# A second token half prepared behind four output sums: a transformer layer on one Trainium2 core

## The chip, the core and the metric

The kernel runs on one core of one Trainium2 chip. The metric is device time in microseconds of one execution. Engines are named as in the profile: PE (TensorE, matmuls and transposes), PEld (its weight loads), DVE (VectorE), ACT (ScalarE), POOL (GpSimd), SP (SyncE); the last two and ACT also issue DMAs. L124 is line 124 of the kernel before.

## The reference

One encoder layer over 1024 tokens of width 1024, in float32:

```python
h   = x + concat(windowed attention, gated delta rule)(rmsnorm(x) @ w_in) @ w_out
hn  = rmsnorm(h, norm_ffn_w)
h   = h + square(relu(hn @ w_ffn_in)) @ w_ffn_out      # 1024 -> 4096 -> 1024
out = rmsnorm(h, norm_final_w)
```

The change lies between the product with `w_out` and the first products of the feed-forward part, and in the last rows of the final norm. What comes before is not touched.

## The kernel before

**Numbers.** Every float32 operand of a large product is split into a high and a low part (a cast on ACT, then a subtraction on POOL or DVE), and a product is three matmuls (`mm3`, L124, L125, L126) that add into one PSUM bank of 128x512. There are eight banks: four named psA and four named psB.

**Output sums.** Tokens are cut into eight chunks of 128. `out_all` walks them from 7 down to 0. For each, `out_gdn` prepares the gated part (four squares L899, small steps L901 to L905, a scaled copy L906, four small transposes L909, a product with the weight L910, a split L119 and L120), `out_gemm` multiplies it with `w_out` (24 matmuls into two psA banks) and adds it to the chunk's rows `h[c]` (L875), and the rows are saved to DRAM as `hd[c]` (L925) and appended to `summed`.

**Token halves.** The feed-forward products are formed in the Strassen-Winograd way: tokens, inner width and columns are each cut in two, and seven products P1 to P7 stand in for eight. The token operand has eight blocks of 128 inner columns per token half: upper blocks k = 0 to 3 and lower blocks 4 to 7. B11 and B21 are the first half's upper and lower blocks, b12 and B22 the second half's. The combinations T3, N1, T2 and N4 are made from them. `norm_rows` gets a chunk's rows ready (a square with its sum on ACT L203, 1/root on POOL L190 and L191, a scaling on DVE L205). `token_block` transposes one block of four chunks into one psB bank (L209), and `split_rows` reads the bank twice (ACT L214, DVE L215). `operand` splits a combination (ACT L948, then POOL or DVE L949).

`tokens_second` does the second half (chunks 4 to 7): per k an upper block, copied to b12 (L963), and a lower one, split to B22 and combined to T3 (L969). `tokens_first` does the first half (chunks 0 to 3): per k an upper block (B11, then N1 = block - b12 at L983), two additions in SBUF that make T2 (L987, L988), then the lower block (B21, and N4 = block - T2 at L991).

**Columns.** `columns` loads two blocks of `w_ffn_in` for a group of 256 columns, forms the sums S1 to S4 and splits what each product needs. Groups 0 and 1 are early ones: P7 and P3, which need only the second half, are taken at once, and the rest later by `rest`. Group 0's raw weights and sums share tiles.

**Order.** A scheduler sets each engine's order from the order in which the code is written and from its own model of times; `weave` mixes generators by weights. In `output`, chunk sums run alone until six are done, then the rest of the sums is mixed with `tokens_second`. Then the first half's rows are normalised, group 1's columns are taken, and the early products are mixed with `tokens_first`. After that, all 16 column groups and the second feed-forward product run in steady state.

**End.** `second_products` adds the last products to the rows of the output and calls `finish` for each of them (square L1212, 1/root, scaling L1215, save L1216). Row 7's last half goes through `finish_last` (L1196 to L1206), which works on half rows and saves them from two queues.

Of the kernel before, what the change touches and what calls it, by code (L numbers as in the profile page):

```python
# [77 lines left out]
class Block:  # L78
# [852 lines left out]
    def norm_h(self, c):  # L931
        self.rows[c] = self.norm_rows(self.h[c], self.sc((P, D)))

# [19 lines left out]
    def tokens_second(self):  # L953

        nc = self.nc
        self.norm_half(1)
        yield 0.5
        rows = [self.rows[4 + i] for i in range(4)]
        self.b12 = []
        for k in range(4):  # L960
            ps = self.token_block(rows, k)
            b12 = self.pt()
            nc.scalar.activation(out=b12, in_=ps, func=AF.Copy, scale=self.w_ffn[:, k:k + 1])  # L963
            self.b12.append(b12)
            yield 0.5
            ps = self.token_block(rows, 4 + k)
            self.split_rows(ps, self.w_ffn, 4 + k, self.X["B22"])
            t3 = self.pt()
            nc.vector.scalar_tensor_tensor(out=t3, in0=ps, scalar=self.w_ffn[:, 4 + k:5 + k], in1=b12, op0=ALU.mult,  # L969
                                           op1=ALU.subtract)  # L970
            self.operand("T3", t3, k % 2)
            yield 0.5

    def tokens_first(self):

        nc = self.nc
        rows = [self.rows[i] for i in range(4)]
        w = self.w_ffn
        for k in range(4):
            ps = self.token_block(rows, k)  # L980
            self.split_rows(ps, w, k, self.X["B11"])
            n1, t2, n4 = self.pt(), self.pt(), self.pt()
            nc.vector.scalar_tensor_tensor(out=n1, in0=ps, scalar=w[:, k:k + 1], in1=self.b12[k], op0=ALU.mult,  # L983
                                           op1=ALU.subtract)
            yield 0.5
            b22 = self.X["B22"][k]
            nc.vector.tensor_tensor(out=t2, in0=n1, in1=b22[:, 0].bitcast(F32), op=ALU.add)  # L987
            nc.vector.tensor_tensor(out=t2, in0=t2, in1=b22[:, 1].bitcast(F32), op=ALU.add)  # L988
            ps = self.token_block(rows, 4 + k)
            self.split_rows(ps, w, 4 + k, self.X["B21"])  # L990
            nc.vector.scalar_tensor_tensor(out=n4, in0=ps, scalar=w[:, 4 + k:5 + k], in1=t2, op0=ALU.mult,  # L991
                                           op1=ALU.subtract)
            self.operand("T2", t2, False)
            self.operand("N1", n1, False)
            self.operand("N4", n4, True)
            yield 0.5

    def load_w1(self, g):
# [5 lines left out]

    def columns(self, raws, early=False):

# [16 lines left out]
        if early:  # L1023
            take("P7")
        take("P1", "P2")
        a["S2"], a["S4"] = a["A11"], a["A12"]
        v.scalar_tensor_tensor(out=a["S2"], in0=a["S1"], scalar=-1.0, in1=a["A11"], op0=ALU.mult, op1=ALU.subtract)
# [133 lines left out]
    def second_products(self, n, p, left, right, banks, last):  # L1161
# [5 lines left out]
        for i in range(4):  # L1167
# [15 lines left out]
            if last and p == "P6":  # L1183
                for d in (self.h[i][:, hi], self.h[4 + i][:, hi], self.h[4 + i][:, lo]):
                    nc.gpsimd.tensor_tensor(out=d, in0=d, in1=u2, op=ALU.add)
            if last and p in ("P3", "P4"):
                self.finish(i if p == "P3" else 4 + i)

    def finish_last(self, t, ps):
# [5 lines left out]
        scr, hw, o = self.pt((P, HALF), BF16), [self.pt(), self.pt()], [self.pt(), self.pt()]  # L1195
        nc.scalar.activation(out=scr, in_=h[:, hi], func=AF.Square, accum_out=ss[:, 1:2])  # L1196
        nc.gpsimd.tensor_tensor(out=hw[1], in0=h[:, hi], in1=self.w_fin[:, hi], op=ALU.mult)
        nc.vector.tensor_tensor(out=h[:, lo], in0=h[:, lo], in1=ps, op=ALU.add)
        nc.scalar.activation(out=scr, in_=h[:, lo], func=AF.Square, accum_out=ss[:, 0:1])
        nc.vector.tensor_tensor(out=hw[0], in0=h[:, lo], in1=self.w_fin[:, lo], op=ALU.mult)  # L1200
        nc.vector.tensor_tensor(out=ss[:, 0:1], in0=ss[:, 0:1], in1=ss[:, 1:2], op=ALU.add)
        self.rstd(ss[:, 0:1], rs)
        nc.scalar.activation(out=o[0], in_=hw[0], func=AF.Copy, scale=rs)
# [33 lines left out]
    def phases(self):  # L1237
# [42 lines left out]
        def output():  # L1280
            yield from self.attention()
            yield from self.out_attn()
            cols[0], rest[0] = self.columns(self.load_w1(0), True)
            out = self.out_all(range(NT - 1, -1, -1))
            while len(self.summed) < 6:
                yield next(out)
            yield from weave((out, 20.0), (self.tokens_second(), 12.0))
# [7 lines left out]
        self.norm_half(0)  # L1295
        cols[1], rest[1] = self.columns(self.load_w1(1), True)
        run(weave((chain(self.early(cols[0]), self.early(cols[1])), 10.0), (self.tokens_first(), 12.0)))
# [23 lines left out]
        for g in range(ng):  # L1321
            then = {}
            if g == 0:
                rest[1]("P6", "P5", "P4")
            elif g + 1 < ng:
                cols[g + 1] = self.columns(self.load_w1(g + 1))
            else:
                w2[0] = self.load_second(0, 0)
                then = {"P2": lambda: prepare(0), "P6": after_p6, "P3": after_p3}
# [31 lines left out]
```

## Time and profile before

| | us |
|---|---|
| median of three runs | 1262.61 |
| lowest and highest run | 1261.38, 1266.63 |
| profiled execution | 1267.07 |
| its span from first to last instruction | 1265.4 |
| PE busy | 1210.0 (96%) |
| DVE, ACT, POOL busy | 859.0, 621.4, 577.7 |

The granted clock of PE over the whole span was 0.983 of full speed. Times of single instructions below are of the profiled execution, in us from its start. In a row of the trace stand start, duration, engine, line, operation, and what it writes and reads; in brackets the idle time before it and the instruction that ended it. Duration of a pipelined matmul is longer than the distance between two starts.

The output sums of the last chunks end at about 605, the first half's blocks at about 645. The first feed-forward product ends at about 905, the second at 1257, and the rest to 1265.4 is the final norm.

### The profile page before, as it was taken

How to read it: one execution, taken by the hardware profiler on the slowest of the kernel's cores; microseconds unless marked ns; L12 is line 12 of the kernel's file. 1: busy time of each engine (PE TensorE's matmuls, PEld its weight loads, DVE VectorE, ACT ScalarE, POOL GpSimd, SP SyncE). 2: the span in 40 equal slices, each digit the busy share in tenths (PEclk: the TensorE clock that was granted, in tenths of full speed). 3: DMA queues.
4: the chain of work that ended last, by engine and by line, in shares of the span. 5: the costliest groups of instructions: out<-in, count | busy, mean ns of one | idle time of the engine just before them, and what ended most of it. 6: DMA issues, size and time to landing. Idle time of an engine off the chain costs nothing.

```text
span 1265.4 us, 18552 instructions
## 1 busy us (share of the span) xinstructions
PE 1210.0 (96%) x6482; PEld 970.6 (77%) x6482; DVE 859.0 (68%) x1534; ACT 621.4 (49%) x1347; POOL 577.7 (46%) x486
## 2 busy tenths in 40 slices
PE   6999999999899999999799999999999999999997
PEld 5778777778767778878578787887777888888885
DVE  5667666882378987684774544545577897887976
ACT  6455688244475653122654544545545444443443
POOL 5354221352422324143565535445354665565595
PEclk9999999899889999999999999999999999999999
DMA  6134444332956658224034443444687624434233
GB/s 236 51 120 136 111 156 156 122 124 55 229 146 162 174 181 324 68 82 134 18 125 142 153 163 132 152 142 156 204 278 280 220 102 166 150 113 155 85 99 133
DMA packets 121630, 187.62 MB, mean 148 GB/s; under 512 B 11043, under 2 KB 64416, under 8 KB 121537
## 3 DMA queue, kind: packets, MB, share of 16 engines
q1 hardware_dynamic: 96708, 152.58, 37.4%
q10 hardware_dynamic: 16381, 29.67, 6.2%
q0 software_dynamic: 8448, 4.20, 1.8%
q8 instruction: 51, 0.84, 0.3%
q14 instruction: 42, 0.34, 0.1%
HBM read 122.39 MB, written 63.49 MB: 147 GB/s over the span
## 4 chain that ended last, share of the span: by engine, by line
PE 58%; DVE 7%; DMA 3%; issue 2%; POOL 1%; ACT 1%; ACTq 0%; POOLq 0%; DVEq 0%
PE psA L124 8%; PE psA L125 8%; PE psA L126 8%; PE psB L126 7%; PE psB L124 7%; PE psB L125 7%; PE psB L796 5%; DMA pg<-sd 2%; PE psA L584 2%; PE psA L573 2%; DVE pg L1137 1%; PE psA L544 1%; DVE pt L1146 1%; POOL pg L120 1%; PE psA L545 1%
## 5 line engine op out<-in xcount | busy, mean ns | idle before, releaser
L124 PE MATMUL psA<-pg,wh 128*128 128x512 f32 x416 | 167.9, 404 | 2.7 <-ACT pt L458 2.2
L126 PE MATMUL psA<-pg,wl 128*128 128x512 f32 x416 | 167.0, 401 | 0.0
L125 PE MATMUL psA<-pg,wh 128*128 128x512 f32 x416 | 166.6, 400 | 0.3 <-POOL pg L949 0.3
L120 POOL TENSOR_TENSOR wl<-wr,wh 128x512 fp32r<-128x512 f32 x44 | 70.7, 1629 | 153.3 <-ACT wh L119 153.2
L1137 DVE TENSOR_TENSOR pg<-pg 128x512 fp32r<-128x512 f32 x112 | 123.2, 1135 | 18.1 <-ACT pg L1136 18.1
L120 POOL TENSOR_TENSOR wh<-wr,wh 128x512 fp32r<-128x512 f32 x32 | 47.6, 1508 | 132.1 <-ACT wh L119 124.4
L1054 ACT ACTIVATE pt<-pt 128x512 f32<-128x512 f32 x64 | 40.4, 632 | 123.0 <-DVE pt L1044 123.0
L125 PE MATMUL psA<-pg,pg 128*128 128x512 f32 x256 | 99.8, 391 | 0.4 <-POOL pg L120 0.4
L124 PE MATMUL psA<-pg,pg 128*128 128x512 f32 x256 | 99.0, 391 | 0.9 <-DVE pg L1182 0.9
L126 PE MATMUL psA<-pg,pg 128*128 128x512 f32 x256 | 99.7, 389 | 0.0
L120 POOL TENSOR_TENSOR pg<-wr,pg 128x512 fp32r<-128x512 f32 x48 | 73.4, 1559 | 50.8 <-ACT pg L119 50.8
L124 PEld LDWEIGHTS psA<-pg,wh 128*128 128x128 f32 x416 | 79.3, 191 | 22.1 <-ACT pt L458 2.4
L125 PEld LDWEIGHTS psA<-pg,wh 128*128 128x128 f32 x416 | 79.2, 190 | 20.4 <-issue 0.9
L126 PEld LDWEIGHTS psA<-pg,wl 128*128 128x128 f32 x416 | 79.1, 190 | 18.5
L1136 ACT CAST pg<-pg 128x512 fp32r<-128x512 f32 x112 | 66.8, 620 | 38.4 <-DMA pg<-sd 32.0
L125 PE MATMUL psB<-pg,pg 128*128 128x512 f32 x192 | 75.8, 395 | 1.5 <-POOL pg L120 1.4
L126 PE MATMUL psB<-pg,pg 128*128 128x512 f32 x192 | 75.7, 394 | 1.2 <-DVE pg L1137 1.2
L124 PE MATMUL psB<-pg,pg 128*128 128x512 f32 x192 | 75.3, 393 | 0.7 <-ACT pg L1136 0.7
L119 ACT CAST wh<-wr 128x512 fp32r<-128x512 f32 x76 | 43.5, 623 | 45.2 <-PE psA L125 23.6
L1044 DVE TENSOR_TENSOR pt<-psB,pt 128x512 f32<-128x512 f32 x39 | 26.9, 689 | 52.7 <-PE psB L126 30.3
L1044 DVE TENSOR_TENSOR pt<-psA,pt 128x512 f32<-128x512 f32 x39 | 26.7, 689 | 52.8 <-PE psA L126 37.4
L124 PEld LDWEIGHTS psA<-pg,pg 128*128 128x128 f32 x256 | 48.0, 188 | 12.6 <-DVE pg L1182 2.2
(379 smaller groups left out, 3329.5 us busy)
## 6 DMA issues: line engine op xcount, KB each, us to landing
sd<-pt ACTq DMA_DIRECT2D x112, 256.0 KB, 2.1
pg<-sd SPq DMA_DIRECT2D x112, 256.0 KB, 2.8
wr<-in_w_ffn_in SPq DMA_DIRECT2D x32, 512.0 KB, 3.7
wr<-in_w_in SPq DMA_DIRECT2D x22, 512.0 KB, 4.9
pg<-in_x SPq DMA_DIRECT2D x16, 512.0 KB, 4.6
wr<-in_w_ffn_out SPq DMA_DIRECT2D x16, 512.0 KB, 4.9
sc<-kvd SPq DMA_DIRECT2D x14, 512.0 KB, 4.4
kvd<-pt SPq DMA_DIRECT2D x16, 256.0 KB, 2.8
```

The costliest lines, as they stand in the source:

```text
L119: nc.scalar.copy(out=h, in_=raw)
L120: (eng or nc.gpsimd).tensor_tensor(out=l, in0=raw, in1=h.bitcast(F32), op=ALU.subtract)
L124: nc.tensor.matmul(ps, wh, xh, start=first, stop=False, skip_group_check=onto)
L125: nc.tensor.matmul(ps, wh, xl, start=False, stop=False, skip_group_check=onto)
L126: nc.tensor.matmul(ps, wl, xh, start=False, stop=last, skip_group_check=onto)
L573: nc.tensor.transpose(ps[:, g, :], tiles[g // 2][:, g % 2, j * P:(j + 1) * P], self.ident)
L584: nc.tensor.matmul(ps[64 * kv:64 * kv + 64, :], self.va[:, kb, 64 * kv:64 * kv + 64], pts[kv][j].rearrange("p g q -> p (g q)"), start=j == ...
L796: nc.tensor.matmul(ps[:, h - g.start, :], left(h), right[:, h, :], start=True, stop=True)
L1044: self.nc.vector.tensor_tensor(out=out, in0=in0, in1=in1, op=ALU.add)
L1054: self.nc.scalar.activation(out=c, in_=c, func=AF.Relu)
L1136: nc.scalar.copy(out=s[:, 0], in_=raw)
L1137: v.tensor_tensor(out=s[:, 1], in0=raw, in1=s[:, 0].bitcast(F32), op=ALU.subtract)
```

## The change

Four parts.

1. In `output`, the second half joins the sums when four are done (chunks 7 to 4, all that it needs). Its rows are normalised in place in `h` instead of in a copy, so the scaling has to come after the save to DRAM. b12 and t3 of one k lie in one tile of double width and are kept.
2. `tokens_first` takes all four upper blocks first. T2 is made from PSUM and the kept t3 in one pass. The lower blocks follow, and the splits of N4 come last, alternately on POOL and DVE.
3. For group 1, S2 and S4 get tiles of their own, and the splits for P1 and P2 move to the later call.
4. Row 6's `finish` moves into `finish_last`, behind row 7's 1/root; the 1/root of row 7 is made from two partial sums on POOL.

```diff
--- before.py
+++ after.py
@@ -929,7 +929,7 @@
 
 
     def norm_h(self, c):
-        self.rows[c] = self.norm_rows(self.h[c], self.sc((P, D)))
+        self.rows[c] = self.norm_rows(self.h[c], self.sc((P, D)) if c < 4 else None)
 
     def norm_half(self, half):
         for c in range(4 * half + 3, 4 * half - 1, -1):
@@ -956,19 +956,20 @@
         self.norm_half(1)
         yield 0.5
         rows = [self.rows[4 + i] for i in range(4)]
-        self.b12 = []
+        self.b12, self.t3 = [], []
         for k in range(4):
+            both = self.pg((P, 2, HALF))
+            b12, t3 = both[:, 0], both[:, 1]
             ps = self.token_block(rows, k)
-            b12 = self.pt()
             nc.scalar.activation(out=b12, in_=ps, func=AF.Copy, scale=self.w_ffn[:, k:k + 1])
-            self.b12.append(b12)
             yield 0.5
             ps = self.token_block(rows, 4 + k)
             self.split_rows(ps, self.w_ffn, 4 + k, self.X["B22"])
-            t3 = self.pt()
             nc.vector.scalar_tensor_tensor(out=t3, in0=ps, scalar=self.w_ffn[:, 4 + k:5 + k], in1=b12, op0=ALU.mult,
                                            op1=ALU.subtract)
             self.operand("T3", t3, k % 2)
+            self.b12.append(b12)
+            self.t3.append(t3)
             yield 0.5
 
     def tokens_first(self):
@@ -976,24 +977,27 @@
         nc = self.nc
         rows = [self.rows[i] for i in range(4)]
         w = self.w_ffn
+        t2, n4 = [], []
         for k in range(4):
             ps = self.token_block(rows, k)
             self.split_rows(ps, w, k, self.X["B11"])
-            n1, t2, n4 = self.pt(), self.pt(), self.pt()
+            n1, t = self.pt(), self.pt()
+            nc.vector.scalar_tensor_tensor(out=t, in0=ps, scalar=w[:, k:k + 1], in1=self.t3[k], op0=ALU.mult, op1=ALU.add)
             nc.vector.scalar_tensor_tensor(out=n1, in0=ps, scalar=w[:, k:k + 1], in1=self.b12[k], op0=ALU.mult,
                                            op1=ALU.subtract)
+            self.operand("N1", n1, False)
+            t2.append(t)
             yield 0.5
-            b22 = self.X["B22"][k]
-            nc.vector.tensor_tensor(out=t2, in0=n1, in1=b22[:, 0].bitcast(F32), op=ALU.add)
-            nc.vector.tensor_tensor(out=t2, in0=t2, in1=b22[:, 1].bitcast(F32), op=ALU.add)
+        for k in range(4):
             ps = self.token_block(rows, 4 + k)
             self.split_rows(ps, w, 4 + k, self.X["B21"])
-            nc.vector.scalar_tensor_tensor(out=n4, in0=ps, scalar=w[:, 4 + k:5 + k], in1=t2, op0=ALU.mult,
+            n4.append(self.pt())
+            nc.vector.scalar_tensor_tensor(out=n4[k], in0=ps, scalar=w[:, 4 + k:5 + k], in1=t2[k], op0=ALU.mult,
                                            op1=ALU.subtract)
-            self.operand("T2", t2, False)
-            self.operand("N1", n1, False)
-            self.operand("N4", n4, True)
+            self.operand("T2", t2[k], False)
             yield 0.5
+        for k in range(4):
+            self.operand("N4", n4[k], k % 2)
 
     def load_w1(self, g):
         return self.load_w(self.w_cols(self.io["w_ffn_in"][0], 256 * g, 256))
@@ -1002,7 +1006,8 @@
                 "P5": ("S1", "N1", "sc"), "P7": ("S3", "T3", "wh"), "P3": ("S4", "B22", "wl"),
                 "P4": ("A22", "N4", "sc")}
 
-    def columns(self, raws, early=False):
+    def columns(self, raws, early=0):
+
 
 
         nc, v = self.nc, self.nc.vector
@@ -1022,8 +1027,11 @@
         v.tensor_tensor(out=a["S3"], in0=a["A11"], in1=a["A21"], op=ALU.subtract)
         if early:
             take("P7")
-        take("P1", "P2")
-        a["S2"], a["S4"] = a["A11"], a["A12"]
+        if early == 2:
+            a["S2"], a["S4"] = self.pt((P, 4, P)), self.pt((P, 4, P))
+        else:
+            take("P1", "P2")
+            a["S2"], a["S4"] = a["A11"], a["A12"]
         v.scalar_tensor_tensor(out=a["S2"], in0=a["S1"], scalar=-1.0, in1=a["A11"], op0=ALU.mult, op1=ALU.subtract)
         v.tensor_tensor(out=a["S4"], in0=a["A12"], in1=a["S2"], op=ALU.subtract)
         if early:
@@ -1183,7 +1191,7 @@
             if last and p == "P6":
                 for d in (self.h[i][:, hi], self.h[4 + i][:, hi], self.h[4 + i][:, lo]):
                     nc.gpsimd.tensor_tensor(out=d, in0=d, in1=u2, op=ALU.add)
-            if last and p in ("P3", "P4"):
+            if last and p in ("P3", "P4") and (p, i) != ("P4", 2):
                 self.finish(i if p == "P3" else 4 + i)
 
     def finish_last(self, t, ps):
@@ -1194,12 +1202,15 @@
         ss, rs = self.small((P, 2)), self.small((P, 1))
         scr, hw, o = self.pt((P, HALF), BF16), [self.pt(), self.pt()], [self.pt(), self.pt()]
         nc.scalar.activation(out=scr, in_=h[:, hi], func=AF.Square, accum_out=ss[:, 1:2])
+        nc.gpsimd.tensor_scalar(out=ss[:, 1:2], in0=ss[:, 1:2], scalar1=1.0 / D, scalar2=EPS, op0=ALU.mult, op1=ALU.add)
         nc.gpsimd.tensor_tensor(out=hw[1], in0=h[:, hi], in1=self.w_fin[:, hi], op=ALU.mult)
         nc.vector.tensor_tensor(out=h[:, lo], in0=h[:, lo], in1=ps, op=ALU.add)
         nc.scalar.activation(out=scr, in_=h[:, lo], func=AF.Square, accum_out=ss[:, 0:1])
         nc.vector.tensor_tensor(out=hw[0], in0=h[:, lo], in1=self.w_fin[:, lo], op=ALU.mult)
-        nc.vector.tensor_tensor(out=ss[:, 0:1], in0=ss[:, 0:1], in1=ss[:, 1:2], op=ALU.add)
-        self.rstd(ss[:, 0:1], rs)
+        nc.gpsimd.tensor_scalar(out=ss[:, 0:1], in0=ss[:, 0:1], scalar1=1.0 / D, scalar2=ss[:, 1:2], op0=ALU.mult,
+                                op1=ALU.add)
+        nc.gpsimd.tensor_tensor(out=rs, in0=ss[:, 0:1], in1=self.nhalf_exp[:, :1], op=ALU.pow)
+        self.finish(6)
         nc.scalar.activation(out=o[0], in_=hw[0], func=AF.Copy, scale=rs)
         nc.vector.tensor_scalar(out=o[1], in0=hw[1], scalar1=rs, scalar2=None, op0=ALU.mult)
         for i, sl in enumerate((lo, hi)):
@@ -1280,9 +1291,9 @@
         def output():
             yield from self.attention()
             yield from self.out_attn()
-            cols[0], rest[0] = self.columns(self.load_w1(0), True)
+            cols[0], rest[0] = self.columns(self.load_w1(0), 1)
             out = self.out_all(range(NT - 1, -1, -1))
-            while len(self.summed) < 6:
+            while len(self.summed) < 4:
                 yield next(out)
             yield from weave((out, 20.0), (self.tokens_second(), 12.0))
 
@@ -1293,7 +1304,7 @@
                          self.scan(1, tt[1], w_gdn)), 95.0)))
         ng = DFF // 256
         self.norm_half(0)
-        cols[1], rest[1] = self.columns(self.load_w1(1), True)
+        cols[1], rest[1] = self.columns(self.load_w1(1), 2)
         run(weave((chain(self.early(cols[0]), self.early(cols[1])), 10.0), (self.tokens_first(), 12.0)))
         rest[0]("P6", "P5", "P4")
         steps = [(n, p) for n in range(ng // 4) for p in SECOND]
@@ -1321,7 +1332,7 @@
         for g in range(ng):
             then = {}
             if g == 0:
-                rest[1]("P6", "P5", "P4")
+                rest[1]("P1", "P2", "P6", "P5", "P4")
             elif g + 1 < ng:
                 cols[g + 1] = self.columns(self.load_w1(g + 1))
             else:
```

TensorE has the same matmuls and transposes as before. What moves is shown at three places, as each engine's list of instructions (line, operation, output and inputs with the tile's number; the line numbers are those of the kernel that the list is from).

PE at the end of chunk 3's sum, first before, then changed. pg_5261, pg_5165, pg_5076 and pg_4973 are the rows of chunks 4, 5, 6 and 7; psA_5984 and psA_6046 are the bank of chunk 2's sum, pt_5870 and pt_5871 its split operand.

```order
L126 MATMUL psA_5943<-pg_5039,pt_5816 128x512
L909 MATMUL psA_5974<-ident,wr_5959 128x128 x4
L124 MATMUL psA_5984<-pg_5224,pt_5870 128x512
L125 MATMUL psA_5984<-pg_5225,pt_5870 128x512
L126 MATMUL psA_5984<-pg_5224,pt_5871 128x512
L124 MATMUL psA_5984<-pg_4936,pt_5870 128x512
```

```order
L126 MATMUL psA_5943<-pg_5039,pt_5816 128x512
L209 MATMUL psB_5986<-ident,pg_5261 128x128
L209 MATMUL psB_5986<-ident,pg_5165 128x128
L209 MATMUL psB_5986<-ident,pg_5076 128x128
L209 MATMUL psB_5986<-ident,pg_4973 128x128
L209 MATMUL psB_5992<-ident,pg_5261 128x128
...
L209 MATMUL psB_6112<-ident,pg_5076 128x128
L209 MATMUL psB_6112<-ident,pg_4973 128x128
L909 MATMUL psA_6036<-ident,wr_6021 128x128 x4
L124 MATMUL psA_6046<-pg_5224,pt_5870 128x512
```

All 32 transposes of the second half stand behind chunk 3's sum, ahead of the small transposes and the sum of chunk 2; before, they stood further back among the matmuls.

ACT at the same place in the changed kernel. The first row casts chunk 1's gated part, L203 squares the rows of chunks 7 to 3, L899 are chunk 0's four squares, and L964 copies an upper block to b12.

```order
L119 CAST pt_5925<-wr_5903 128x512
L203 ACTIVATE pt_5959,sm_5957<-pg_4973 128x1024
L203 ACTIVATE pt_5966,sm_5964<-pg_5076 128x1024
L203 ACTIVATE pt_5973,sm_5971<-pg_5165 128x1024
L203 ACTIVATE pt_5980,sm_5978<-pg_5261 128x1024
L203 ACTIVATE pt_6015,sm_6013<-pg_5350 128x1024
L899 ACTIVATE scr_6025,sm_6023<-pg_3794 128x128 x2
L964 ACTIVATE pg_5985<-psB_5986,cols 128x512
L899 ACTIVATE scr_6025,sm_6023<-pg_3794 128x128
L214 ACTIVATE pg_5997<-psB_5992,cols 128x512
L899 ACTIVATE scr_6025,sm_6023<-pg_3794 128x128
```

The squares of the second half follow the cast directly, and chunk 0's preparation lies between the first evictions.

DVE in the first half, before (one k) and changed (upper blocks). In the changed kernel L985 makes T2 and L986 makes N1, and pg_5985 and pg_6004 hold the kept b12 and t3.

```order
L215 SCALAR_TENSOR_TENSOR pg_6287<-psB_6282,cols,pg_6287 128x512
L983 SCALAR_TENSOR_TENSOR pt_6290<-psB_6282,cols,pt_6098 128x512
L215 SCALAR_TENSOR_TENSOR pg_6301<-psB_6296,cols,pg_6301 128x512
L987 TENSOR_TENSOR pt_6291<-pt_6290,pg_6128 128x512
L988 TENSOR_TENSOR pt_6291<-pt_6291,pg_6128 128x512
L991 SCALAR_TENSOR_TENSOR pt_6292<-psB_6296,cols,pt_6291 128x512
L949 TENSOR_TENSOR pg_6311<-pt_6292,pg_6311 128x512
L215 SCALAR_TENSOR_TENSOR pg_6319<-psB_6314,cols,pg_6319 128x512
```

```order
L215 SCALAR_TENSOR_TENSOR pg_6243<-psB_6238,cols,pg_6243 128x512
L985 SCALAR_TENSOR_TENSOR pt_6247<-psB_6238,cols,pg_5985 128x512
L986 SCALAR_TENSOR_TENSOR pt_6246<-psB_6238,cols,pg_5985 128x512
L215 SCALAR_TENSOR_TENSOR pg_6258<-psB_6253,cols,pg_6258 128x512
L985 SCALAR_TENSOR_TENSOR pt_6262<-psB_6253,cols,pg_6004 128x512
L986 SCALAR_TENSOR_TENSOR pt_6261<-psB_6253,cols,pg_6004 128x512
L215 SCALAR_TENSOR_TENSOR pg_6273<-psB_6268,cols,pg_6273 128x512
L985 SCALAR_TENSOR_TENSOR pt_6277<-psB_6268,cols,pg_6072 128x512
```

Before, a k had two L215, N1, two additions, N4 and a split; now an upper block has three passes over the same bank. On ACT the changed order there is:

```order
L214 ACTIVATE pg_6243<-psB_6238,cols 128x512
L948 CAST pg_6250<-pt_6246 128x512
L214 ACTIVATE pg_6258<-psB_6253,cols 128x512
...
L948 CAST pg_6265<-pt_6261 128x512
L214 ACTIVATE pg_6273<-psB_6268,cols 128x512
L948 CAST pg_6280<-pt_6276 128x512
L214 ACTIVATE pg_6288<-psB_6283,cols 128x512
L948 CAST pg_6295<-pt_6291 128x512
```

The cast of N1 (L948) stands ahead of the next block's first eviction (L214).

DVE in the last rows, before and changed (L1215 and L1226 are the scaling of a row in `finish`, L1200 and L1209 the product with the norm's weight in `finish_last`):

```order
L1182 TENSOR_TENSOR pg_8769<-pg_8769,psA_11070 128x512
L1215 SCALAR_TENSOR_TENSOR wr_11255<-pg_8768,sm_11250,wl_10676 128x1024
L1198 TENSOR_TENSOR pg_8770<-pg_8770,psA_11084 128x512
L1215 SCALAR_TENSOR_TENSOR wr_11277<-pg_8769,sm_11272,wl_10676 128x1024
L1200 TENSOR_TENSOR pt_11295<-pg_8770,wl_10676 128x512
L1201 TENSOR_TENSOR sm_11292<-sm_11292 128x1
L1204 TENSOR_SCALAR pt_11298<-pt_11296,sm_11293 128x512
```

```order
L1190 TENSOR_TENSOR pg_8759<-pg_8759,psA_11060 128x512
L1226 SCALAR_TENSOR_TENSOR wr_11245<-pg_8758,sm_11240,wl_10666 128x1024
L1207 TENSOR_TENSOR pg_8760<-pg_8760,psA_11074 128x512
L1209 TENSOR_TENSOR pt_11276<-pg_8760,wl_10666 128x512
L1215 TENSOR_SCALAR pt_11279<-pt_11277,sm_11274 128x512
L1226 SCALAR_TENSOR_TENSOR wr_11294<-pg_8759,sm_11289,wl_10666 128x1024
```

Row 6's scaling, which stood between row 7's sum and its product, is now the last one.

## The prediction

> **What bounds the kernel now.** I read the page first (busy shares), then the waits of TensorE by stage, then the instructions in time order around the place that the change touches, then the granted clock there and the last rows.
>
> ```profile
> PE 1210.0 (96%) x6482; PEld 970.6 (77%) x6482; DVE 859.0 (68%) x1534; ACT 621.4 (49%) x1347; POOL 577.7 (46%) x486
> ```
>
> TensorE is the bound: 96% of the span. A change that leaves its instructions alone can gain only where it idles or runs slowly. The order of TensorE's instructions differs in one stretch, from the end of chunk 3's output sum (585.11) to product P1 of column group 2 (660.98). Its rows, its windows (us, busy of PE, PEld, DVE, ACT, POOL, then granted clock, DMA share, GB/s) and TensorE's waits in it:
>
> ```profile
> 585.46 0.48 PE L124 MATMUL psA<-pg,pt 128*128 128x512 f32 x1
> ...
> 600.19 1.91 PE L209 MATMUL psB<-ident,sc 128*128 128x128 f32 x16
> 601.85 0.47 PE L124 MATMUL psA<-pg,pt 128*128 128x512 f32 x1
> ```
> ```profile
> 585.11:609.00 23.89, 23.89 (x123) 19.59 (x121) 13.28 (x20) 11.80 (x21) 8.70 (x13) 1.00 0.38 133
> 609.00:640.00 31.00, 21.38 (x86) 14.58 (x86) 24.94 (x34) 19.39 (x35) 21.77 (x19) 0.89 0.10 31
> 640.00:660.80 20.80, 20.80 (x92) 16.84 (x91) 13.19 (x18) 10.25 (x19) 10.35 (x8) 1.00 0.38 130
> ```
> ```profile
> PE psB L124 <- DVE pt L983: 2.5, 1, 2.5
> PE psB L209 <- DVE pt L991: 2.1, 1, 2.1
> PE psB L209 <- DVE sc L205: 2.0, 2, 1.2
> PE psA L124 <- ACT wl L119: 1.4, 1, 1.4
> ```
>
> Between 585.46 and 600.19 stand 63 matmuls, 0.234 us each; sixteen transposes take 1.66, 0.104 each. The stretch holds 228 matmuls, 64 transposes and a group of four small ones (0.35): 53.3 + 6.7 + 0.35 = 60.3 us of work in 75.9. So 15.5 us are lost, and that is all the change can win there. Idle are 9.6 (31.00 − 21.38), all between 609 and 640, where the first token half is evicted from PSUM; DVE is busy 24.94 of those 31. The clock of 0.89 costs 3.4 more (31 × 0.11); the other 2.5 are stretched matmuls beside transposes and short waits. From 585 to 609 TensorE loses nothing visible: second-half preparation lies beside the output sums.
>
> **Second half after four sums.** The 32 transposes of the second half move from between later matmuls to one block right behind chunk 3's sum, ahead of chunks 2, 1 and 0. The first of them reads chunk 4, the last normalised. On ACT the four squares (L203) follow a cast (L119) that waited for DVE until 580.68.
>
> ```profile
> 580.68 0.62 ACT L119 CAST pt<-wr 128x512 fp32r<-128x512 f32 x1 [5.32 <-DVE wr L910]
> ...
> 593.17 1.05 ACT L203 ACTIVATE pt<-pg 128x1024 bf16<-128x1024 f32 x1
> 594.13 0.19 ACT L203 ACTIVATION_READ_ACCUMULATOR pt<-pg 128x1 f32 x1
> ```
> ```profile
> 589.71 0.75 POOL L190 TENSOR_SCALAR sm<-sm 128x1 f32<-128x1 f32 x1
> ...
> 594.73 0.19 POOL L190 TENSOR_SCALAR sm<-sm 128x1 f32<-128x1 f32 x1
> 595.01 0.55 POOL L191 TENSOR_TENSOR sm<-sm,nhalf_exp 128x1 f32<-128x1 f32 x1
> ```
> ```profile
> 595.59 0.75 DVE L205 TENSOR_SCALAR sc<-pg,sm 128x1024 f32<-128x1024 f32 x1 [0.79 <-POOL sm L191]
> ```
>
> Squares start at 581.2 and, at 1.05 each, end at 585.4. From the accumulator's end (594.32) to the normalised row (596.34) the trace has 2.0. So the row is ready at 587.4, and TensorE, done at 585.11, idles 2.3. POOL's small L190 took 0.75 beside a running L205 instead of 0.19; with two such hits, and a queue behind the split of group weights, it is up to 3.7. I take 3.0 (gap A). Before, gap A was hidden by chunks 3 to 0, 15 us of matmuls; that cover is now behind the transposes in TensorE's queue.
>
> Normalising in place makes L205 wait for the save of the row to DRAM:
>
> ```profile
> 580.01 0.33 SPq L925 DMA_DIRECT2D hd<-pg  x1
> ```
> ```profile
> hd<-pg SPq DMA_DIRECT2D x8, 512.0 KB, 3.0
> ```
>
> The save of chunk 4 lands at 583.0, over 3 us ahead of its L205 (586.7): nothing. Were it as late as 588, chunks 5 to 7 would be behind it on DVE, and gap A would grow by 1.
>
> Eight blocks of transposes follow each other on four psB banks, with no matmul between. Block b5 needs b1's bank back, and so on; each needs the ACT copy and two DVE passes:
>
> ```profile
> 601.41 0.68 ACT L214 ACTIVATE pg<-psB,cols 128x512 fp32r<-128x512 f32 x1
> ```
> ```profile
> 602.13 0.75 DVE L215 SCALAR_TENSOR_TENSOR pg<-psB,cols,pg 128x512 fp32r<-128x512 f32 x1 [1.75 <-ACT pg L214]
> 602.79 0.74 DVE L969 SCALAR_TENSOR_TENSOR pt<-psB,cols,pt 128x512 f32<-128x512 f32 x1
> ```
> ```profile
> L899 ACT ACTIVATE scr<-pg x32: 303/310/313, 473.4 to 572.2; 128x128 f32<-128x128 f32 x32
> ```
>
> b6 waits for DVE on b2, b8 for DVE on b4. ACT has chunk 0's four L899 among them (0.31 each, some 0.44 with the accumulator read, 0.19, partly beside it), and DVE four small L901 to L904. Pairs follow at some 2.0 (ACT: 0.58 + 0.58 + cast 0.52 + L899 0.44). Four pairs, 8.0 us from the first transpose to the first matmul of chunk 2, hold 3.7 of work: 4.3 lost (gap B; 3.3 without the L899, 4.9 with every DVE op in the way). This too was covered by matmuls before.
>
> The shared slot for b12 and t3 takes no instruction. DVE's normalisation in place reads and writes the same bytes: nothing.
>
> **First half by upper blocks.** T2 comes from one pass over PSUM with t3 (L985) in place of two SBUF additions (L987, L988): four DVE passes fewer, net of what N4 shifts. Order on DVE is now L215, L985, L986 per upper block, and ACT goes L948 (cast N1 of block k), then L214 of block k+1: the next eviction waits for L986 of this one. Cycle: cast 0.52, L214 0.69, DVE 3 × 0.66 + 0.08, hand-overs 0.08: 3.35 per upper block. Four take 13.4, and four lower ones at about 1.4 (two DVE passes; their cast is early) 5.6: 19.0. Before, the cycle is read from L983, once per k:
>
> ```profile
> 618.58 0.74 DVE L983 SCALAR_TENSOR_TENSOR pt<-psB,cols,pt 128x512 f32<-128x512 f32 x1
> ...
> 632.04 0.73 DVE L983 SCALAR_TENSOR_TENSOR pt<-psB,cols,pt 128x512 f32<-128x512 f32 x1
> ...
> 639.60 0.73 DVE L983 SCALAR_TENSOR_TENSOR pt<-psB,cols,pt 128x512 f32<-128x512 f32 x1
> ```
>
> Three cycles take 21.0, 7.0 each: four are 28.0, 9.0 more.
>
> TensorE, though, has little to do meanwhile. From 585.11 it has gaps A and B (7.3), 36 transposes (3.7) and 98 matmuls (22.9) before this half's first block: 619.0. The eviction of b1 begins at 619.9, so b4's bank is free only at 619.9 + 13.4 less the first cast = 632.7. The blocks b1 to b4 and the 22 matmuls behind them last to 625.8; then all four lower blocks stand in one row of transposes, 1.7, done at 627.5 without waits, and b8 waits for 632.7: 5.2 (gap C; 3.9 with b7's wait partly before, 5.6). Then P1's 12 matmuls and P2's first nine (4.9) cover the lower evictions but for the last: 1.2, with a little for POOL's low parts (gap D; 0 to 4.0). POOL's price depends on what DVE does meanwhile:
>
> ```profile
> 632.54 1.30 POOL L120 TENSOR_TENSOR sc<-wr,sc 128x512 fp32r<-128x512 f32 x1
> 633.79 1.73 POOL L120 TENSOR_TENSOR sc<-pt,sc 128x512 fp32r<-128x512 f32 x1
> ```
> ```profile
> 633.35 1.03 DVE L987 TENSOR_TENSOR pt<-pt,pg 128x512 f32<-128x512 f32 x1
> ```
>
> POOL now gets 12 low parts instead of 10 (N4 two, no longer all on DVE). I take 1.45 per row, near the 1.30, which stands beside DVE's PSUM pass of 632.04; most DVE passes beside the new low parts read PSUM too. The Trainium skill, "SBUF — State Buffer", section "SBUF: two separate sides", has DVE and GpSimd exclude each other for a whole instruction when DVE has two SBUF inputs; L985 has one. The 1.73, beside the SBUF addition at 633.35, agrees. It speaks for the change, and would leave gap D at 0.7.
>
> **Group 1's sums in slots.** S2 and S4 of group 1 get their own tiles, so P1 and P2 splits of group 1 may come after P3's. The same casts and subtractions, moved later; they lie beside group 0's products, 20.8 us with no idle in the third window. Zero; at most 1.4 (the ACT wl L119 wait) either way.
>
> **Clock.** Idle of about 2 us halves the clock in this trace:
>
> ```profile
> 948.00:950.00 2.00, 1.04 (x4) 1.00 0.93 329
> 950.00:952.00 2.00, 0.73 (x2) 1.00 0.95 265
> 952.00:954.00 2.00, 1.94 (x6) 0.74 0.93 331
> 954.00:956.00 2.00, 2.00 (x6) 0.50 0.79 316
> 956.00:958.00 2.00, 2.00 (x9) 0.91 0.36 137
> ```
>
> There 2.2 idle in 4 us cost (0.26 + 0.50 + 0.09) × 2 = 1.7; the stretch 609 to 640 cost 3.4 for its 9.6. Gaps A with B and gap C each make such a pause: 1.25 each to 1.7, together 2.5 (0 to 5.5). The Trainium skill ("TensorE: Matmul & The Clock Gate", section "What's actually happening") has the clock fall after at least one idle window of some 3.4 us; the rows show it falling with 1.04 and 0.73 busy in neighbouring windows, so a full idle window isn't needed here.
>
> **Last rows.** finish(6) now comes behind row 7's factors; row 6's product (L1215) no longer stands between row 7's on DVE.
>
> ```profile
> 1257.12 0.69 DVE L1198 TENSOR_TENSOR pg<-pg,psA 128x512 f32<-128x512 f32 x1 [0.83 <-PE psA L126]
> 1257.73 1.83 DVE L1215 SCALAR_TENSOR_TENSOR wr<-pg,sm,wl 128x1024 f32<-128x1024 f32 x1
> 1259.49 0.68 DVE L1200 TENSOR_TENSOR pt<-pg,wl 128x512 f32<-128x512 f32 x1
> ...
> 1261.93 0.34 ACTq L1206 DMA_DIRECT2D out<-pt  x1
> ```
>
> Row 7: square ends 1258.6, POOL 0.19 + 0.55 and hand-overs, 1259.5; its halves leave at about 1260.5. Row 6: its square (1.06) follows row 7's on ACT, accumulator at 1259.85, POOL 0.8 → 1260.65, product 1.28 uncontended → 1261.95. So the last issue is at 1261.95 instead of 1261.93, with 512 KB instead of 256: +0.2 (−0.3 to +0.9).
>
> **The sum.** Lost after: 3.0 + 4.3 + 5.2 + 1.2 + 2.5 + 1.3 (stretched matmuls, half of the 2.5, as transposes now stand in blocks) = 17.5, against 15.5: +2.0, and +0.2 at the end: +2.2. The profiled execution took 1267.07 (span 1265.4), so 1269.3 by its own clock; it lies 4.5 above the median 1262.61, so the median becomes 1264.8. Low ends (2.3, 3.3, 3.9, 0, 0, 0.5, −0.3) give 9.7, −5.8; high ends (3.7, 4.9, 5.6, 4.0, 5.5, 2.5, 0.9) 27.1, +11.6, not likely together.
>
> **Rivals.** What can be told from no change here is 0.5%, 6.3 us.
>
> 1. *Likeliest, 0.55:* idle only moves from the first half to the second; 1264.8, own range 1261 to 1268.
> 2. *Faster, 0.25:* DVE bounded the first half, and 9.0 us less chain there (28.0 − 19.0) closes gaps C and D but for 1.1, with one clock fall less. 17.5 − 5.3 − 1.25 = 10.9 against 15.5: −4.6, 1258.2; with gaps A and B at their low ends −6.3, 1256.3. DVE's 24.94 of 31 speaks for it; against it, that only 22 matmuls stand between b4 and b5, so that no faster DVE than 13.4 us for four blocks fills them.
> 3. *Slower, 0.15:* POOL. At 1.74 each rather than 1.45 the 12 low parts and the six splits of group 0 take 5.2 more, of which 3.5 to 4 would be on P6, P5 and P4, which come last; with one clock fall more (1.7), which makes +7.6: 1270.2. It decides from about 1.6 per row on; against it, DVE's PSUM operands.
> 4. *The clock stays full, 0.05:* the Trainium skill's rule taken as it stands (TensorE page, above): none of gaps A to D reaches 3.4 without a transpose in it. Worked from rows, the term of 2.5 is 0: 1262.3.
>
> Faster by over 0.5% is half of rival 2 with a little for the likeliest: 0.14. Slower by over 0.5% (above 1268.9) is most of rival 3 and the likeliest's upper end: 0.17. The same: 0.69. The range 1257 to 1271 leaves a tenth at each end.
>
> **What would show it.** After: TensorE idle right behind chunk 3's sum, waiting for L205 (gap A), then for L968 among the transposes (B). L215, L985, L986 in cycles of 3.3, waits of psB transposes for them (C). POOL rows of 1.3 to 1.5 at N4, clock at 0.5 in the windows after the pauses, row 6's product last. Wrong if TensorE runs through the first blocks (rival 2's gain and more), or if P5, P6 or P4 wait for POOL by over 3 us.

## The result and the profile after

The changed kernel is slower: 1271.11 us in the median of six runs (1269.15 to 1275.17), against 1263.55 for the kernel before on the same chip. The ratio is 1.0064 (95% interval 1.005 to 1.0078). The forecast was 1264.8 with a range to 1271.0 and "no change" as the likeliest; the time lies 0.1 above the range. A repeat of the changed kernel in a second session (a_again, below) gave 1.0053 (1.0036 to 1.007).

The profiled execution took 1272.02 (span 1270.1). Three marks cut it. The first is the group of small transposes L909 ahead of chunk 3's sum, the last place where both orders agree. The second is the first matmul of the second feed-forward product (the first `psA<-pg,pg`), since the first feed-forward product runs without idle and at full clock behind the changed part. The third is the last matmul. Rows of the trace, before first (`...` stands for rows left out, here and below):

```profile
579.10 0.60 PE L909 MATMUL psA<-ident,wr 128*128 128x128 f32 x4
...
919.80 0.40 PE L124 MATMUL psA<-pg,pg 128*128 128x512 f32 x1
...
1256.70 0.39 PE L126 MATMUL psA<-pg,pg 128*128 128x512 f32 x1
```
```profile
580.28 0.60 PE L909 MATMUL psA<-ident,wr 128*128 128x128 f32 x4
...
926.01 0.40 PE L124 MATMUL psA<-pg,pg 128*128 128x512 f32 x1
...
1260.94 0.39 PE L126 MATMUL psA<-pg,pg 128*128 128x512 f32 x1
```

From mark one to mark two, called the stretch below, before took 340.70 and after 345.73: +5.0. The second product took 336.90 and 334.93, the rest to the end 8.70 and 9.16. The differences ahead of mark one (1.2) and in the second product (2.0) are not put down to the change: the fourteen profiles of this study spread by 4.7 and 4.4 there.

TensorE's work is what it was (6482 instructions); its share of the span fell from 96% to 95%:

```profile
PE 1212.7 (95%) x6482; PEld 976.0 (77%) x6482; DVE 851.5 (67%) x1527; ACT 621.5 (49%) x1347; POOL 579.1 (46%) x489
```

Its waits from 580 to 680 (us in total, times, longest), and the rows in time order behind which they stand:

```profile
PE psB L209 <- DVE pt L986: 6.2, 3, 2.7
PE psB L209 <- DVE pg L205: 3.6, 1, 3.6
PE psB L124 <- DVE pt L995: 1.6, 1, 1.6
PE psB L209 <- DVE pg L968: 1.5, 1, 1.5
PE psB L209 <- ACT pg L964: 0.5, 1, 0.5
```
```profile
590.04 4.75 PE L209 MATMUL psB<-ident,pg 128*128 128x128 f32 x24 [3.58 <-DVE pg L205]
595.31 0.66 PE L209 MATMUL psB<-ident,pg 128*128 128x128 f32 x4 [0.52 <-ACT pg L964]
597.42 1.09 PE L209 MATMUL psB<-ident,pg 128*128 128x128 f32 x4 [1.46 <-DVE pg L968]
...
630.89 0.63 PE L209 MATMUL psB<-ident,sc 128*128 128x128 f32 x4 [0.87 <-DVE pt L986]
634.24 0.72 PE L209 MATMUL psB<-ident,sc 128*128 128x128 f32 x4 [2.72 <-DVE pt L986]
637.58 1.09 PE L209 MATMUL psB<-ident,sc 128*128 128x128 f32 x4 [2.62 <-DVE pt L986]
```

These are gaps A (3.58), B (0.52 + 1.46 = 1.98), C (0.87 + 2.72 + 2.62 = 6.21) and D (1.6): 13.4 us of idle where before had 9.5. The cycle behind gap C shows in the rows of DVE and ACT. DVE starts the four upper blocks at equal distances, and ACT has a cast and then its next eviction between two of them:

```profile
625.33 0.75 DVE L215 SCALAR_TENSOR_TENSOR pg<-psB,cols,pg 128x512 fp32r<-128x512 f32 x1 [1.80 <-ACT pg L214]
...
635.37 0.75 DVE L215 SCALAR_TENSOR_TENSOR pg<-psB,cols,pg 128x512 fp32r<-128x512 f32 x1 [1.27 <-ACT pg L214]
```
```profile
627.43 0.62 ACT L948 CAST pg<-pt 128x512 fp32r<-128x512 f32 x1 [2.14 <-DVE pt L986]
627.96 0.68 ACT L214 ACTIVATE pg<-psB,cols 128x512 fp32r<-128x512 f32 x1
```

(635.37 − 625.33) / 3 is 3.35 a block, as forecast. DVE waits 1.27 of it for ACT, and ACT 2.14 for DVE.

The second half has the same pattern. There ACT's cast of T3 (L948) waits for DVE and stands ahead of the next upper block's copy to b12 (L964):

```profile
591.02 0.69 ACT L964 ACTIVATE pg<-psB,cols 128x512 f32<-128x512 f32 x1 [1.47 <-PE psB L209]
...
594.05 0.62 ACT L948 CAST pg<-pg 128x512 fp32r<-128x512 f32 x1 [1.19 <-DVE pg L968]
594.58 0.68 ACT L964 ACTIVATE pg<-psB,cols 128x512 f32<-128x512 f32 x1
...
597.84 0.68 ACT L964 ACTIVATE pg<-psB,cols 128x512 f32<-128x512 f32 x1
```

The pairs of blocks follow each other at 3.56 and 3.26.

The rest is the clock. The windows are chosen so that each holds one state (us, PE busy, granted clock, DMA share, GB/s), after first and then the one fall of before in this place:

```profile
586.87:590.28 3.41, 0.24 (x2) 1.00 0.38 154
590.28:593.70 3.42, 3.42 (x18) 0.50 0.00 0
593.70:597.11 3.41, 1.69 (x12) 1.00 0.00 0
597.11:600.52 3.41, 3.10 (x12) 0.50 0.00 0
600.52:603.94 3.42, 3.42 (x16) 1.00 0.61 178
...
631.24:634.66 3.42, 0.70 (x7) 1.00 0.00 0
634.66:638.07 3.41, 0.79 (x5) 0.50 0.00 0
638.07:641.48 3.41, 1.81 (x6) 0.50 0.00 0
641.48:644.90 3.42, 3.42 (x9) 0.50 0.00 0
644.90:648.31 3.41, 3.41 (x16) 1.00 0.59 169
```
```profile
632.12:638.95 6.83, 6.03 (x14) 0.50 0.31 89
```

After, TensorE is busy for 3.42 + 3.10 + 0.79 + 1.81 + 3.42 = 12.5 us at half clock, which cost 6.3; before 6.03, which cost 3.0. So the part of the stretch that was forecast (75.9 us before, 81.2 after) lost 13.4 idle, 6.3 by the clock and 1.2 that is left over (stretched matmuls): 20.9, where before had 15.5.

### The profile page after: what moved, and what is told of

Its sections match the earlier page's. It is cut to its first block, busy times and chain, and to the rows that moved or that the text cites. A ratio compares the mean times of both kernels' runs of the same rounds, so it can differ in the third digit from the quotient of the medians.

```text
span 1270.1 us, 18546 instructions
## 1 busy us (share of the span) xinstructions
PE 1212.7 (95%) x6482; PEld 976.0 (77%) x6482; DVE 851.5 (67%) x1527; ACT 621.5 (49%) x1347; POOL 579.1 (46%) x489
## 5 line engine op out<-in xcount | busy, mean ns | idle before, releaser
L124 PEld LDWEIGHTS psA<-pg,pg 128*128 128x128 f32 x256 | 48.0, 188 | 13.2 <-DVE pg L1190 2.2
```

The costliest lines, as they stand in the source:

```text
L124: nc.tensor.matmul(ps, wh, xh, start=first, stop=False, skip_group_check=onto)
```

## The experiments

**Theory 1:** the second half started early costs, because its transposes stand uncovered on TensorE; idle alone and the clock that falls behind it make the loss. **Theory 2:** the first half by upper blocks costs, and the early start takes off more than it adds. Each part was done or undone by itself. Times are medians, ratios are to the kernel before on the same chip.

| kernel | ratio (95%) | stretch | tail |
|---|---|---|---|
| before | 1 | 340.70 | 8.70 |
| changed | 1.0064 (1.005 to 1.0078) | 345.73 | 9.16 |
| changed, again (a_again) | 1.0053 (1.0036 to 1.007) | 346.71 | 9.14 |
| changed, join at six sums (a_six) | 1.0008 (0.9995 to 1.002) | 343.39 | 9.14 |
| before with part 1 (b_early) | 1.0057 (1.0038 to 1.0076) | 347.79 | 8.63 |
| before with part 2 (b_first) | 0.999 (0.9974 to 1.0006) | 339.62 | 8.61 |
| before with part 3 (b_cols2) | 1.0006 (0.9995 to 1.0018) | 342.31 | 8.72 |
| before with part 4 (b_tail) | 1.0001 (0.9986 to 1.0017) | 340.61 | 9.14 |
| changed without part 3 (a_cols1) | 1.0032 (1.0016 to 1.0047) | 343.92 | 9.16 |
| changed, cast moved (a_pipe) | 0.9995 (0.9981 to 1.0009) | 339.89 | 9.16 |
| changed, idle filled (a_warm2) | 1.0031 (1.0018 to 1.0045) | 343.82 | 9.10 |
| b_first, cast moved (b_first_pipe) | 0.9984 (0.9971 to 0.9997) | 340.17 | 8.69 |
| changed without part 4, cast moved, idle filled (pipe_warm) | 0.9993 (0.9979 to 1.0007) | 337.85 | 8.68 |
| parts 2 and 3, rows in place, cast moved (b_parts23_pipe) | 0.9947 (0.9927 to 0.9967) | 333.96 | 8.70 |

The stretch and the tail are of one profile each, in us. The stretch came within 0.1 in the two kernels of one order there (before, b_tail), within 1.0 in the changed one and its repeat.

**The early start, undone and alone.** The early join of part 1 undone in the changed kernel, its rows still in place (a_six), and part 1 done alone (b_early):

```diff
-            while len(self.summed) < 4:
+            while len(self.summed) < 6:
```
```diff
-        self.rows[c] = self.norm_rows(self.h[c], self.sc((P, D)))
+        self.rows[c] = self.norm_rows(self.h[c], self.sc((P, D)) if c < 4 else None)
...
-            while len(self.summed) < 6:
+            while len(self.summed) < 4:
```

> The changed kernel with one number put back: the second token half joins the output sums when six are done, not four; everything else stays changed. Theory 1 (the early start costs): the row of 32 transposes right behind chunk 3's sum made 5.6 us of idle in the profile after (3.58 for L205, 0.52, 1.46) and a fall of the clock worth 3.0; both go, so 8.6 less than the changed kernel's 1271.1: about 1262.5, that is -0.1% against the kernel before. Theory 2 (the first half by upper blocks costs): the 6.2 + 1.6 of idle before the lower blocks with its clock fall stay, and the second half, now later, delays the first half as well: 1268 or more, +0.4% against before.

> The kernel before with part 1 alone: join at four sums, rows normalised in place; tokens_first, columns and last rows as before. Theory 1: the 5.6 us of idle and one clock fall (3.0) are added to what the first half lost before: 1263.5 + 8.6 = about 1272 (+0.65%). Theory 2: the early start costs little by itself, since it takes work off the first half's time: 1263 to 1266.

Theory 1 stands: 1264.91 without the early start, 1271.44 with it alone. Alone, it shows the same wait of 3.58, and then one longer than any in the changed kernel, for chunk 0's preparation (L906), which stands behind the evictions:

```profile
587.83 6.20 PE L209 MATMUL psB<-ident,pg 128*128 128x128 f32 x28 [3.58 <-DVE pg L205]
598.44 1.11 PE L909 MATMUL psA<-ident,wr 128*128 128x128 f32 x4 [4.41 <-DVE wr L906]
```

In a_six TensorE is never idle from 583 to 605, where b_early has 14.01 busy of 22 at a clock of 0.69:

```profile
583.00:605.00 22.00, 22.00 (x113) 1.00 0.40 144
```
```profile
583.00:605.00 22.00, 14.01 (x53) 0.69 0.19 59
```

a_six did not come to the 1262.5 that I had expected: its first half still waited 7.7 for L986, with two falls of the clock in the stretch.

**Part 2 and part 4 alone.** For part 2 `tokens_second` keeps t3 and `tokens_first` is the new one; for part 4 `finish_last` is the new one and row 6 is taken out of the earlier call.

> The kernel before with part 2 alone: t3 kept, T2 from PSUM in one pass, upper blocks first, N4 splits last; joined at six sums as before. Theory 1: idle of 7.8 and 2.9 for the clock in place of 9.5 and 3.0: 1263.5 - 1.8 = about 1262 (-0.1%). Theory 2: the order of upper blocks, with ACT and DVE taking turns at 3.35 us a block, costs 4 more: 1267 to 1268 (+0.3%).

> The kernel before with part 4 alone, the order of the last rows. From the two profiles the stretch from the last matmul to the end is 8.7 before and 9.2 after: +0.5 us, 1264.0 (+0.04%). Theory 2: part 4 explains some of what the profiles leave open between +4.7 (profiled) and +7.5 (medians): +2 or more, 1265.5.

Part 2 gave 1262.62; the interval holds 1, so the small gain that theory 1 expected isn't shown, but the loss of theory 2 is ruled out. Part 4 is too small for the runs, but all seven profiles with it have a tail of 9.10 to 9.16, and all seven without it 8.61 to 8.72: +0.45.

**Part 3.** a_cols1 takes it out of the changed kernel, b_cols2 adds it to the one before, and a_again repeats the changed kernel beside it:

```diff
-        cols[1], rest[1] = self.columns(self.load_w1(1), 2)
+        cols[1], rest[1] = self.columns(self.load_w1(1), 1)
...
-                rest[1]("P1", "P2", "P6", "P5", "P4")
+                rest[1]("P6", "P5", "P4")
```

> The changed kernel without part 3: group 1's sums share tiles again, P1 and P2 split early. Theory 1 (part 3 is worth nothing): 1271 to 1272, same as the changed kernel. Theory 2: it takes casts away from the first half's ACT, and without it the first half loses up to 1.4 more: 1272.5.

> The kernel before with part 3 alone: slots for group 1's S2 and S4, its P1 and P2 split later. Theory 1: nothing, 1264 within 1.5. Theory 2: part 3 costs 3 to 4 by itself: 1267.5 (+0.3%).

> The changed kernel once more, beside kernels of the same session. Its profile accounts for +5.0 us in the stretch from chunk 3's sum to the second feed-forward product and +0.5 in the last rows, 5.5 in all (+0.44%), but its median was 7.5 above (+0.64%), while the kernel without part 3 came out at +0.32%. Theory 1 (the missing 2 us are the chance of where clock falls land, not part 3): +0.3 to +0.5% here. Theory 2 (part 3 costs some 4 us): +0.64% again.

Without part 3 the changed kernel was at 1268.03, better than either theory said; on the kernel before, part 3 came out as nothing, 1265.79. The repeat's 0.53% lies between its two theories, and its interval holds both. Idle from 585 to 690 is 13.2 in a_cols1, 13.4 and 14.4 in the two profiles of the changed kernel. The larger difference is the clock in the first half: it is low for 6.8 us in a_cols1 and for 10.2 in the other two. TensorE's order differs too: in a_cols1 the first lower block's transposes stand ten matmuls earlier. Whether part 3, that order or the position of the pause makes the difference is open; the intervals of a_cols1 and a_again overlap.

**The cast behind the next eviction.** In `tokens_first` the split of N1 of block k is written after `split_rows` of block k + 1. No instruction is added.

```diff
-            self.operand("N1", n1, False)
+            if n1s:
+                self.operand("N1", n1s.pop(), False)
+            n1s.append(n1)
```

> The changed kernel with the cast of N1 of block k (L948 on ACT) written behind the eviction of block k+1 (L214) instead of ahead of it; no work is added or taken away. Theory 1 (the first half loses because ACT and DVE take turns, 3.35 us a block): the cycle falls to DVE's three passes, about 2.1, four blocks take 8.4 instead of 13.4, the 6.2 of idle before the lower blocks falls to about 1.2 and the clock does not fall there (-2.9): 1271.1 - 7.9 = about 1263. Theory 2 (the blocks wait for TensorE's banks and POOL, not for ACT's order): within 1 us of 1271.

1264.1: 7 us won by one line's place. TensorE's order is the changed kernel's up to product P1, behind gap D. DVE's upper blocks in a_pipe:

```profile
621.67 0.75 DVE L215 SCALAR_TENSOR_TENSOR pg<-psB,cols,pg 128x512 fp32r<-128x512 f32 x1 [1.80 <-ACT pg L214]
...
623.65 0.74 DVE L215 SCALAR_TENSOR_TENSOR pg<-psB,cols,pg 128x512 fp32r<-128x512 f32 x1
...
627.61 0.74 DVE L215 SCALAR_TENSOR_TENSOR pg<-psB,cols,pg 128x512 fp32r<-128x512 f32 x1
```

The four blocks follow at 1.98, three passes with no wait for ACT, and L986's 6.2 in TensorE's waits became 2.4. One part of the expectation failed: the clock fell here all the same, for 6.83 us behind a window with 1.26 of busy time.

**Idle filled.** 24 transposes of the identity ahead of the second half's first block and 16 ahead of its fourth; they add instructions and no result.

```diff
+        for i in range(warm):
+            self.nc.tensor.transpose(ps[:, 0:P], self.ident, self.ident)
...
-            ps = self.token_block(rows, k)
+            ps = self.token_block(rows, k, 24 if k == 0 else 0)
...
-            ps = self.token_block(rows, 4 + k)
+            ps = self.token_block(rows, 4 + k, 16 if k == 1 else 0)
```

> The changed kernel with idle filled: 24 transposes of the identity (2.5 us) ahead of the second half's first block and 16 (1.7) ahead of its fourth, written into the same banks and overwritten. They lie in the 3.58 and 2.0 us in which TensorE waited. Theory 1 (idle makes the clock fall): the two falls between 589 and 601, 3.0 us together, go or shrink to one: 1271.1 - 1.5 to -3 = about 1268.5 to 1269.5, with the granted clock near 1.00 from 585 to 605. Theory 2 (the falls come by chance or by the kind of work): the clock falls as before, and the time is 1271 to 1272.5.

1268.77. The same 17 us counted from mark one, a_warm2 first, then the changed kernel:

```profile
580.18:597.18 17.00, 13.93 (x97) 1.00 0.09 33
```
```profile
584.00:601.00 17.00, 11.38 (x53) 0.80 0.11 42
```

With work that computes nothing in the pauses, both falls are gone: idle is the cause of these two. Their price shows in the profile: the stretch is 1.9 shorter, though the normalised rows come no earlier. In the medians it is 0.2 to 0.3%, and the intervals of a_warm2 and a_again still overlap a little.

**Together.** Three combinations:

> The kernel before with part 2 alone (upper blocks first) and the cast of N1 written behind the next block's eviction. In the run with part 2 alone TensorE idles 6.4 in the first half and the clock falls to 0.73 in the stretch from 609 to 640. Theory 1: 3.1 of idle goes, and with it most of the clock's fall (3 to 6): 1262.6 - 5 = about 1257.5, 0.5% below the kernel before. Theory 2: the clock falls anyway or the waits move to POOL's low parts: 1261 to 1263.

> The changed kernel without part 4, with the cast of N1 moved and the idle before and among the second half's blocks filled with 40 transposes of the identity. Without the filling (and with part 4) the time was that of the kernel before, with two half-clock stretches of 6.8 us. Theory 1 (idle causes the fall, and the early start costs just its gaps): the first stretch goes, -2.5 to -3, and part 4's 0.5: 1261, -0.25%. Theory 2 (the filling delays the blocks or the clock falls anyway): 1264 to 1265.

> The kernel before with rows of the second half normalised in place, parts 2 and 3, and the cast of N1 behind the next block's eviction; joined at six sums, last rows as before. Theory 1: the first half's cycle is 2.0 instead of 3.35 and the second half is covered by the output sums: like part 2 with the cast moved, 1261.5 to 1263, 0.1 to 0.2% below before. Theory 2: part 3 costs 3 to 4: 1266.

b_first_pipe missed: 1263.49, 0.16% below before instead of 0.5%. pipe_warm missed too: 1263.87 instead of 1261, no better than a_pipe by the ratio, though its profile has no fall between 549 and 629 and a stretch 2.0 shorter. Gaps A and B remain in it (3.1 us). So a gain by filling is seen in one pair of kernels and not in the other. b_parts23_pipe is the version that beats both kernels: 1258.58, ratio 0.9947 (0.9927 to 0.9967), more than I had expected of it. Its waits from 580 to 672 and the only fall of the clock in the place:

```profile
PE psB L209 <- DVE pt L986: 2.0, 2, 1.5
PE psA L124 <- ACT wh L119: 1.0, 1, 1.0
PE psB L124 <- DVE pt L999: 0.7, 1, 0.7
PE psB L209 <- DVE sc L205: 0.6, 1, 0.6
PE psA L125 <- DVE pg L949: 0.3, 1, 0.3
```
```profile
622.99:626.40 3.41, 1.25 (x8) 1.00 0.43 133
626.40:629.81 3.41, 2.93 (x7) 0.50 0.06 21
629.81:633.23 3.42, 3.42 (x15) 1.00 0.00 0
```

Idle is 4.6, and 2.93 at half clock cost 1.5. Against b_first_pipe it has part 3 and the rows in place. In its list of TensorE instructions the 12 matmuls of group 1's P3 stand ahead of the lower blocks, in b_first_pipe behind them. That is 2.8 us of cover more, at the place where b_first_pipe waits 5.0 for L986. This order was not tried by itself. The same 12 matmuls bear on the miss of b_first_pipe: in b_first they stand between the third and the fourth lower block. The scheduler moved them together with the cast, so the pair b_first and b_first_pipe doesn't show the cast alone.

Four of these kernels make a square of two choices. They are the changed kernel but for these choices, and b_parts23_pipe also leaves out part 4 (0.45 us, 0.04%):

| ratio to before | cast ahead of the eviction | cast behind it |
|---|---|---|
| joined at four sums | 1.0064, 1.0053 | 0.9995 (a_pipe) |
| joined at six sums | 1.0008 (a_six) | 0.9947 (b_parts23_pipe) |

The early start costs 0.4 to 0.6% in either column, and the cast's place 0.6 to 0.7% in either row. Theory 1 named the first alone; the second costs at least as much.

## Why the prediction was wrong

- **The clock is the step that failed.** The sum had two pauses at 1.25 each, 2.5; measured are three falls and 6.3. I scaled a fall down from the row of the second product (1.7, one window) although the same trace had priced the one at this very place at over 3. What was lost in the stretch is 20.9 instead of 17.5. Of these 3.4, the clock is 3.8, idle −0.3 and the rest −0.1.
- **The second half after four sums.** Gap A: 3.0 forecast, 3.58 measured; the wait, its place and its releaser (L205 of chunk 4) were right. Gap B: 4.3 forecast, 1.98 measured, and its working was wrong twice. Pairs of blocks follow at 3.56 and 3.26, not at 2.0, because ACT and DVE take turns here too; and the last block waits for the second pair, not for four of them. That both errors nearly cancel is luck: from the first transpose to the first matmul of chunk 2 the forecast had 8.0, and it took 8.97 (590.04 to 599.01), 8.03 in a_warm2 at full clock. Less of it is idle because the transposes ran at half clock. A, B and the clock together were 8.8 for 8.55, so the excess is not here. The save of the row to DRAM held nothing up.
- **The first half.** The cycle of 3.35 was exact. Gap C was 6.2 for 5.2, gap D 1.6 for 1.2, and the fall behind them cost 3.0 for 1.25: 10.8 for 7.65. Here lies the excess. Idle in all was 13.4 against 13.7 forecast, though for gap B only by the luck above.
- **The rule beside it.** The Trainium skill ("TensorE: Matmul & The Clock Gate", section "What's actually happening") lets the clock fall after one idle window of about 3.4 us, in a window that runs freely. My fourth rival read from it that no fall would come, but falls came: the windows ahead of them hold 0.24, 1.69 and 0.70 of busy time, so a window need not be empty. The length of the falls agrees with the page: 3.42, 3.41 and 3 × 3.41.
- **The base.** The forecast is the median before and 2.2. That median was 1262.61 in three runs and 1263.55 in six, which is 0.9 of the miss of 6.3; the stretch is 3.4 and the last rows 0.3, and the remaining 1.7 are not located. The repeat leaves no such rest: its stretch is 6.0 longer than before and its tail 0.4, and its median is 6.5 above (1271.43 against 1264.92). The 4.5 us by which the profiled run before lay above its median are not in the stretch: its second product took 336.9, 1.9 above the middle of the fourteen profiles, and mark one came 1.6 later than in their middle.
- **The last rows.** +0.2 forecast, +0.46 measured. Row 6's last issue comes 5.56 behind the last matmul's start instead of 5.25; most of that is its POOL step L190, which took 0.48 for 0.19 beside DVE's scaling for row 7:

```profile
1263.99 0.48 DVE L1215 TENSOR_SCALAR pt<-pt,sm 128x512 f32<-128x512 f32 x1 [1.20 <-POOL sm L1212]
1264.04 0.48 POOL L190 TENSOR_SCALAR sm<-sm 128x1 f32<-128x1 f32 x1
...
1266.50 0.33 SPq L1227 DMA_DIRECT2D out<-wr  x1
```

- **The rivals.** POOL's low parts (rival 3) did not decide: no wait for POOL of the first half's operands shows. Slower came by the likeliest case's own mechanism, with its clock term above its upper end: 6.3, where 5.5 stood. Rival 2 was right that the first half's chain is what counts, and wrong that DVE's passes set it: ACT's order did.

## What to carry to other kernels

Work taken ahead on a queue that runs in order has to be judged by what covered it where it stood: 32 transposes among output sums cost nothing, the same 32 in one row cost 5.6 us of waits and two clock falls. Where two engines take turns on one buffer, look at the order of the smaller one's list: moving a cast behind the next eviction took the cycle from 3.35 to 1.98. That took 7 us off the changed kernel; it gained nothing clear of noise where the order of TensorE changed with it (b_first to b_first_pipe). And price a pause of TensorE as its length and one to three windows at half clock, if it leaves a window of 3.41 us with less than about 1.5 of work.

## What the runs showed of the hardware

The clock falls in steps: every fall in the changed stretch of the fourteen profiles lasted one, two or three windows of 3.41 us, and a window full of work at half clock costs 1.7. The fall goes with TensorE's busy time in the window before. Laid out in such windows from 10 us to the last matmul, all fourteen profiles show a fall behind every window of full clock that held 1.47 or less, and none behind one that held more than 2.38. Between the two it went both ways, within 4 us in the repeat of the changed kernel (a_again):

```profile
583.97:587.38 3.41, 1.48 (x14) 1.00 0.38 154
587.38:590.79 3.41, 1.55 (x13) 1.00 0.00 0
590.79:594.21 3.42, 2.33 (x10) 0.50 0.00 0
```

So busy time alone doesn't decide there; what else does is open. The windows also lie differently in each run: behind mark one, one begins after 10.00 us in the changed kernel's profile, and after 7.84 and 11.25 in the repeat's. The same waits can so cost one window more or less.
